# A decoder trunk on one core: gated-branch and merge-gate chunks of the in-projection as seven block products, the recurrence on 128-channel tiles, and the second branch product first

## The chip, the cores and the metric

The kernel runs on one core of a Trainium2 chip. The metric is the device time of one execution in microseconds, as the median of several runs. A profile of one further execution, taken by the hardware, gives the time of every instruction on every engine: TensorE (PE, and PEld for its weight loads), VectorE (DVE), ScalarE (ACT), GpSimd (POOL) and the queues of the DMA engines, of which SP's and POOL's are used here.

## The reference

One layer, 1024 positions, width 1024, everything in float32. Three branches come out of one wide in-projection; the rest is an output projection and a squared-ReLU MLP.

```python
h = rms_norm(x, g_mix)
z = einsum("bsd,de->bse", h, w_in) + b_in                # 1024 -> 7168
va, ga, xb, gb, sa, sb = split(z)                        # 1024,1024,1536,1536,1024,1024
u = causal_depthwise_conv(va * sigmoid(ga), conv_a_w, conv_a_b)      # width 31
u = silu(layer_norm(u, ln_g, ln_b))
y_a = u @ w_a_out
v = causal_depthwise_conv(xb, conv_b_w, conv_b_b)                    # width 4
r, i = sigmoid(blockdiag(v, w_rg_a) + b_a), sigmoid(blockdiag(v, w_rg_x) + b_x)   # 16 heads of 96
a = exp(-8 * r * softplus(-lam))
bterm = sqrt(1 - a**2) * i * v                           # the root is 1 at position 0
hs[t] = a[t] * hs[t-1] + bterm[t]
y_b = (hs * gelu(gb)) @ w_b_out
x = x + (sigmoid(sa) * y_a + sigmoid(sb) * y_b) @ w_o
x = x + square(relu(rms_norm(x, g_mlp) @ w_1)) @ w_2
return rms_norm(x, g_final)
```

## The kernel before

Activations lie transposed: channels on the 128 partitions, positions along the row, so a tile is 128 channels by 1024 positions (4 KB per partition), and a PSUM bank takes 512 positions. Precision is kept by splitting each operand into a high part in a rounded format (float32r) and a low part, the rest; a product is then three products: high by high, high by low, low by high. `split` makes the parts with a ScalarE copy and a VectorE subtraction; `split_dma` with two ScalarE copies and an accumulating transfer on POOL's queue.

**In-projection.** The 7168 output channels are 56 chunks of 128. `zchunk` loads the chunk's weights (`get_w`, two buffers each of raw, high and low), and `mm3` runs 8 blocks x 3 parts x 2 halves = 48 products of 128x128 by 128x512 into one of three PSUM tiles of two banks. The first three chunks are made beside the first normalization (`first_z`). The order of the others is the order of the program: for j from 0 to 7, three `xb` chunks (while j is below 4), one `va` and one `ga` chunk (`va_pair`), and some merge-gate chunks (`GATES`); then the 12 gated-branch chunks `GB`. `step()` after a chunk advances the recurrence by one unit.

**Recurrence.** A unit is one head (96 channels) and one half of the positions (32 units): `rnn_load` gathers its 96 rows out of the 128-channel tiles by SP's queue, `rnn_split` makes the parts, `rnn_gates` runs 6 products into one PSUM tile (both gates, one half each) and two sigmoids, and `rnn_scan`, per head, does Exp, Tanh and Sqrt on ScalarE and multiplications and the scan on VectorE, and sends the rows back to the 128-channel tile by SP's queue.

**Long convolution.** In `va_pair`, 30 taps of one VectorE instruction each per chunk (L508, with 1024 positions), at a priority lowered by 1500 so that they fill VectorE's gaps.

**After the in-projection.** The layer norm over the eight convolution tiles is spread over the `GB` loop (`layer_norm_steps`, at `LNS`); a `GB` chunk's Gelu is multiplied straight into the recurrence's tile. Then come the first branch product, `ya` (8 chunks of 48), and the second, `yb` (8 chunks of 72), each multiplied by merge gates that lay in DRAM (`spill`); the output projection; the MLP. The MLP's up-projection (`up_mm`, `up_step`) already takes its 2x2 block products by a scheme of seven instead of eight (Strassen's, in Winograd's form), 12 products a step, on a pool of eight single PSUM banks; so does the down-projection.

**Order.** Except where `tc.manual_schedule` fixes the order of PE, ACT and DVE (start, head of the MLP, down-projection), a scheduler lays down each engine's order before the run, by priority (earlier in the program first, `tc.high_priority` ahead), and each engine then runs its queue strictly in that order. Tiles come from pools with a fixed number of slots; `acts`, the largest, has 35 tiles of 4 KB per partition. An instruction that writes a tile waits until the last reader of the slot's former tile is done.

Of the kernel before, what the change touches and what calls it, by code (L numbers as in the profile page):

```python
# [9 lines left out]
F32 = mybir.dt.float32  # L10
F32R = mybir.dt.float32r
# [14 lines left out]
QB = 11  # L26
GATES = (0, 1, 1, 2, 3, 3, 3, 3)
LNS = (3, 4, 6, 8, 9)
# [4 lines left out]
def trunk_kernel(ctx: ExitStack, tc: tile.TileContext, x, xt_in, vecs, w_in, w_a_out, w_b_out,  # L33
# [8 lines left out]
    wp = early.enter_context(tc.tile_pool(name="weights", bufs=2))  # L42
# [27 lines left out]
    def split_w(raw, shape, name, pool=wp, tag=None):  # L70
        wh = pool.tile(shape, F32R, tag=tag or "wh", name=name + "_h")
        wl = pool.tile(shape, F32R, tag=tag or "wl", name=name + "_l")
        split_dma(raw, wh, wl)
        return wh, wl
# [48 lines left out]
    rnn = ExitStack()  # L123
    qp = rnn.enter_context(tc.tile_pool(name="half", bufs=QB))
    vp = rnn.enter_context(tc.tile_pool(name="evac", bufs=2))
    up = rnn.enter_context(tc.tile_pool(name="conv_in", bufs=2))
    rp = rnn.enter_context(tc.tile_pool(name="heads", bufs=2))

    def Q(name, dt=F32, rows=HD):
        return qp.tile([rows, HS], dt, tag="q", name=name)  # L130

    def EV(name):
        return vp.tile([P, HS], F32, tag="ev", name=name)


    vec = cp.tile([P, 452], F32, name="vec")
# [10 lines left out]
    lam_c = vec[0:HD, 404:420]  # L147
    ba_c = vec[0:HD, 420:436]
    bx_c = vec[0:HD, 436:452]
# [34 lines left out]
    xh = [T(f"xh{c}", F32R) for c in range(8)]  # L184
    xl = [T(f"xl{c}", F32R) for c in range(8)]
# [36 lines left out]
    def x_scaled(hf, c):  # L222
        u = xc[4 * hf + c // 2][:, HALVES[c % 2]]
        nc.vector.scalar_tensor_tensor(u, u, gmix_c[:, c:c + 1], rb[hf], ALU.mult, ALU.mult)
        nc.scalar.activation(xh[c][:, HALVES[hf]], u, AF.Copy)

    def x_low(hf, c):
        u, h = xc[4 * hf + c // 2][:, HALVES[c % 2]], xh[c][:, HALVES[hf]]
        nc.vector.tensor_tensor(xl[c][:, HALVES[hf]], u, h.bitcast(F32), ALU.subtract)

    xw = [(wide(xh[k]), wide(xl[k])) for k in range(8)]
# [20 lines left out]
    def first_z(i, hf, k, which):  # L252
        w, a = {"hh": (0, xh), "lh": (1, xh), "hl": (0, xl)}[which]
        nc.tensor.matmul(z0[i][:, HALVES[hf]], w0[i][w][:, k, :], a[k][:, HALVES[hf]],  # L254
# [4 lines left out]
    c8 = cp.tile([HD, NH], F32, name="c8")  # L259
    sm = cp.tile([HD, 8, NH], F32, name="sm")  # L260
    c4 = sm[:, 7, :]

    def decay():
        smi = cp.tile([HD, NH], I32, name="smi")
# [32 lines left out]
    with tc.manual_schedule(engines={mybir.EngineType.Activation, mybir.EngineType.DVE,  # L297
                                     mybir.EngineType.PE}):
        warm = cp.tile([P, 2], F32, name="warm")
        nc.vector.memset(warm, 1.0)  # L300
# [63 lines left out]

    VA, GA, XB, GB, SA, SB = 0, 8, 16, 28, 40, 48
# [17 lines left out]
    hst = vt  # L383
# [17 lines left out]

    gws = {}
    parts = {}

    def rnn_load(hd, hf):
        g, hh = divmod(hd, 4)
        v = Q(f"v{hd}_{hf}")
        for (ti, p0, p1, d0) in PIECES[hh]:
            nc.sync.dma_start(v[d0:d0 + p1 - p0, :], vt[3 * g + ti][p0:p1, HALVES[hf]])
        parts[hd, hf] = [v]  # L410
        if hf == 0:
            raw = rp.tile([HD, 2, HD], F32, tag="rraw", name=f"rraw{hd}")
            if hd < 2:
                nc.gpsimd.tensor_copy(raw[0:1, 0, 0:1], vt[0][0:1, 0:1])
            nc.sync.dma_start(raw, w_rg[hd])
            gws[hd] = raw

    def rnn_split(hd, hf):
        if hf == 0:
            gh = rp.tile([HD, 2, HD], F32R, tag="rh", name=f"rgh{hd}")  # L420
            gl = rp.tile([HD, 2, HD], F32R, tag="rl", name=f"rgl{hd}")
            split(gws[hd], gh, gl)
            gws[hd] = (gh, gl)
        vh = Q(f"vh{hd}_{hf}", F32R)
        vl = Q(f"vl{hd}_{hf}", F32R)
        split_dma(parts[hd, hf][0], vh, vl)
        parts[hd, hf] += [vh, vl]

    def rnn_gates(hd, hf):
        v, vh, vl = parts.pop((hd, hf))  # L430
        gh, gl = gws[hd]
        ps = PS(f"rg{hd}_{hf}", "ps2")
        for gi in range(2):
            o = ps[:HD, HALVES[gi]]
            nc.tensor.matmul(o, gh[:, gi, :], vh, start=True, stop=False)  # L435
            nc.tensor.matmul(o, gl[:, gi, :], vh, start=False, stop=False)  # L436
            nc.tensor.matmul(o, gh[:, gi, :], vl, start=False, stop=True)  # L437
        r = Q(f"r{hd}_{hf}")
        i = Q(f"i{hd}_{hf}")
        nc.scalar.activation(r, ps[:HD, 0:HS], AF.Sigmoid, bias=ba_c[:, hd:hd + 1])  # L440
        nc.scalar.activation(i, ps[:HD, HS:S], AF.Sigmoid, bias=bx_c[:, hd:hd + 1])
        nc.vector.tensor_tensor(i, i, v, ALU.mult)
        return r, i

    def rnn_scan(hd, rs):
        g, hh = divmod(hd, 4)
        if hd < NH - 1:
            at = wide(T(f"a{hd}")[:HD, :])
        else:
            at = [Q(f"a{hd}_{hf}") for hf in range(2)]  # L450
        for hf in range(2):
            r = rs[hf][0]
            nc.scalar.activation(at[hf], r, AF.Exp, scale=c8[:, hd:hd + 1])
            nc.scalar.activation(r, r, AF.Tanh, scale=c4[:, hd:hd + 1])
# [834 lines left out]
```

## Time and profile before

| | |
|---|---|
| time, median of 3 runs (lowest, highest) | 1623.0 us (1622.24, 1624.71) |
| the profiled execution: its time, its span | 1622.71 us, 1620.7 us |
| TensorE products | 7074 |
| busy: PE, DVE, ACT, POOL | 1600.2, 1094.9, 931.0, 179.8 us |
| granted TensorE clock, mean | 0.999 |
| DMA: software queue, hardware queue | 97.24 MB, 147.22 MB |
| end of the in-projection; of `ya`; of `yb` | 678.6, 765.7, 897.2 us |

Busy time is the time in which an engine had at least one instruction running; TensorE's is modelled, since its products overlap in a pipeline, so the count of products in a stretch of time says more. In the window rows, each engine has its busy time and, in brackets, its instructions; then come the granted clock, the share of the 16 DMA engines and GB/s. In the rows of groups, the columns are line, engine, operation, output and inputs with shapes, and count; then busy time and mean ns of one; then the idle time of the engine just before them and what ended most of it.

### The profile page before, as it was taken

What the parts mean: (1) busy time and instruction counts of PE and PEld (TensorE: products, weight loads), DVE (VectorE), ACT (ScalarE), POOL (GpSimd) and SP (SyncE); (2) the same over time, 40 slices, a digit from 0 to 9 for tenths busy, and PEclk for the clock granted to TensorE, in tenths of its full rate; (3) what the DMA queues carried; (4) which work ended last, traced back from release to release, by engine and by line L of the source; (5) the groups of instructions that cost most, each with busy time, mean ns of one, the idle gap of its engine ahead of it and who ended that gap; (6) DMA issues with size and microseconds to landing.
All of it is one profiled execution on the core that took longest, in us unless ns stands there. A gap on an engine that the chain in (4) does not pass through costs nothing.

```text
span 1620.7 us, 18731 instructions
## 1 busy us (share of the span) xinstructions
PE 1600.2 (99%) x7074; PEld 1313.3 (81%) x7074; DVE 1094.9 (68%) x1319; ACT 931.0 (57%) x1185; POOL 179.8 (11%) x244
## 2 busy tenths in 40 slices
PE   8999999999999999999999999999999999999997
PEld 6888888888888887888888888788888888888886
DVE  6699999998989736612312146865555457888898
ACT  5579889999973347722422235654444466555552
POOL 0111111211211100111111100000000001111110
PEclk9999999999999999999999999999999999999999
DMA  7556666766664543464754641633322579889862
GB/s 291 113 127 143 141 153 137 163 152 161 166 143 119 131 92 90 111 189 98 184 137 115 181 156 66 198 116 116 115 104 104 184 231 234 214 215 228 214 130 104
DMA packets 81513, 245.90 MB, mean 152 GB/s; under 512 B 9568, under 2 KB 11104, under 8 KB 81424
## 3 DMA queue, kind: packets, MB, share of 16 engines
q0 software_dynamic: 29392, 97.24, 29.7%
q1 hardware_dynamic: 51888, 147.22, 27.4%
q8 instruction: 55, 0.90, 0.2%
q14 instruction: 34, 0.28, 0.1%
q10 hardware_dynamic: 144, 0.26, 0.0%
HBM read 123.05 MB, written 33.55 MB: 97 GB/s over the span
## 4 chain that ended last, share of the span: by engine, by line
PE 94%; issue 2%; DVE 2%; ACT 1%; DMA 1%; POOL 0%; SPq 0%; POOLq 0%; DVEq 0%; ACTq 0%
PE z L92 33%; PE d L1073 14%; PE yb L92 8%; PE ya L92 5%; PE o L672 3%; PE e L1188 2%; PE keep L1073 2%; PE o L92 2%; PE z L254 2%; PE rg L437 1%; PE rg L435 1%; DMA vl<-v 1%; PE rg L436 1%; PE o L696 1%; PE tr_m L744 0%
## 5 line engine op out<-in xcount | busy, mean ns | idle before, releaser
L508 DVE SCALAR_TENSOR_TENSOR y<-u,vec,y 128x1024 f32<-128x1024 f32 x240 | 307.3, 1281 | 15.8 <-ACT y L504 10.7
L92 PE MATMUL z<-xh,win_h 128*128 128x512 f32 x848 | 262.9, 391 | 0.0
L92 PE MATMUL z<-xl,win_h 128*128 128x512 f32 x848 | 261.8, 390 | 0.0
L92 PE MATMUL z<-xh,win_l 128*128 128x512 f32 x848 | 200.9, 389 | 0.0
L92 PEld LDWEIGHTS z<-xh,win_h 128*128 128x128 f32 x848 | 159.2, 188 | 35.8 <-issue 1.7
L92 PEld LDWEIGHTS z<-xl,win_h 128*128 128x128 f32 x848 | 159.2, 188 | 33.8 <-issue 0.2
L92 PEld LDWEIGHTS z<-xh,win_l 128*128 128x128 f32 x848 | 159.2, 188 | 33.0
L1085 DVE TENSOR_TENSOR acc<-acc,d 128x1024 f32<-128x1024 f32 x72 | 87.8, 1220 | 33.4 <-PE d L1073 32.7
L68 ACT ACTIVATE win_h<-win_raw 128x1024 fp32r<-128x1024 f32 x53 | 55.8, 1055 | 86.3 <-PE z L92 81.0
L67 POOL DMA_DIRECT2D win_l<-win_raw x53 | 46.6, 880 | 336.1 <-ACT win_l L66 299.9
L66 ACT ACTIVATE win_l<-win_raw 128x1024 fp32r<-128x1024 f32 x53 | 55.7, 1050 | 10.0 <-PE z L92 6.1
L635 DVE TENSOR_TENSOR sb<-yb,sb 128x1024 f32<-128x1024 f32 x8 | 9.8, 1224 | 73.8 <-PE yb L92 73.8
L806 ACT ACTIVATE o<-s 128x512 fp32r<-128x512 f32 x64 | 38.1, 621 | 32.6 <-DVE s L798 28.3
L611 DVE TENSOR_TENSOR m<-ya,sa 128x1024 f32<-128x1024 f32 x8 | 9.8, 1224 | 68.8 <-PE ya L92 68.8
L806 ACT ACTIVATE o<-w_raw 128x512 fp32r<-128x512 f32 x40 | 25.0, 624 | 51.4 <-DVE o L720 50.8
L590 DVE TENSOR_TENSOR v<-v,ge 128x512 f32<-128x512 f32 x24 | 16.4, 689 | 47.7 <-ACT ge L588 47.7
L397 DVE SCALAR_TENSOR_TENSOR v<-xb,vec,v 128x1023 f32<-128x1023 f32 (+2 forms) x36 | 45.4, 1272 | 2.2 <-ACT v L392 2.2
L720 DVE TENSOR_TENSOR o<-s,o 128x512 fp32r<-128x512 f32 x64 | 42.4, 685 | 5.9 <-ACT o L806 5.8
L704 DVE TENSOR_TENSOR x<-xr,o 128x1024 f32<-128x1024 f32 x8 | 9.6, 1218 | 51.9 <-PE o L672 37.7
L67 POOL DMA_DIRECT2D db_1l<-wr x7 | 6.1, 870 | 327.4 <-ACT db_1l L66 304.8
L118 ACT ACTIVATE xn<-x 128x1024 f32<-128x1024 f32 x8 | 8.4, 1057 | 58.4 <-DVE x L704 58.4
L92 PE MATMUL ya<-suh,wa_h 128*128 128x512 f32 x128 | 39.4, 389 | 0.0
(1104 smaller groups left out, 3859.5 us busy)
## 6 DMA issues: line engine op xcount, KB each, us to landing
win_raw<-in_w_in_dram SPq DMA_DIRECT2D x53, 512.0 KB, 4.8
win_l<-win_raw POOLq DMA_DIRECT2D x53, 512.0 KB, 4.6
fr<-fd SPq DMA_DIRECT2D x32, 512.0 KB, 5.6
wr<-in_w_dram SPq DMA_DIRECT2D x32, 512.0 KB, 5.9
w_raw<-in_w_dram SPq DMA_DIRECT2D x31, 512.0 KB, 3.4
gates<-s POOLq DMA_DIRECT2D x32, 256.0 KB, 4.3
fd<-fa SPq DMA_DIRECT2D x16, 512.0 KB, 3.1
fd<-fb SPq DMA_DIRECT2D x16, 512.0 KB, 3.2
```

Source lines behind the costliest of these rows:

```text
L66: nc.scalar.activation(l, src, AF.Copy, scale=-1.0)
L67: nc.gpsimd.dma_start(l, src, accum_op=ALU.add)
L68: nc.scalar.activation(h, src, AF.Copy)
L92: nc.tensor.matmul(ps[:, HALVES[hf]], a, b[hf], start=i == 0, stop=i == len(todo) - 1)
L254: nc.tensor.matmul(z0[i][:, HALVES[hf]], w0[i][w][:, k, :], a[k][:, HALVES[hf]], start=k == 0 and which == "hh", stop=k == 7 and which == ...
L397: nc.vector.scalar_tensor_tensor(v[:, d:S], a[:, 0:S - d], cbw_c[:, w * 12 + t:w * 12 + t + 1], v[:, d:S], ALU.mult, ALU.add)
L508: nc.vector.scalar_tensor_tensor(acc, u[:, w:w + S], caw[:, w * 8 + j:w * 8 + j + 1], acc, ALU.mult, ALU.add)
L672: nc.tensor.matmul(ps[:, HALVES[hf]], tok(a, k, t), wo[k][b][:, HALVES[hf]], start=k == 0 and b == 0 and n == 0, stop=k == 7 and b == 1)
L720: tt(l, src, h.bitcast(F32), ALU.subtract)
L806: nc.scalar.activation(o[:, 0], src, AF.Copy)
L1073: nc.tensor.matmul(o, a, b, start=n == 0 and (p != 1 or g == 0), stop=n == len(todo) - 1, skip_group_check=p == 1 and g > 0)
L1085: tt(acc[p, q2], acc[p, q2], ps, ALU.add)
```

## The change

The twelve gated-branch chunks and the sixteen merge-gate chunks leave the loop over j and follow it as a second stage. They are taken in 14 pairs (`ZPAIRS`): a pair of chunks, two halves of the inner dimension and two halves of the positions make a 2x2 block product, done in seven steps (`z_step`, `z_mm`) of 12 products each. The right operands are sums of blocks of the normalized x (`x_sums`), read back from a copy in DRAM (`xu`); the left ones are sums of blocks of the weights (`z_lhs`), five of seven split by `split_dma`. Sums of results are made by copying a PSUM bank into another (ScalarE) and accumulating further products there, and by VectorE additions on the way out. Gelu times the recurrence's output goes to DRAM (`hgd`), merge gates as before (`spill`). PSUM is eight single banks in this stage, and nine weight tiles are shared by raw weights and split operands.

The recurrence takes a whole head (1024 positions) as its unit for the gate products, with one PSUM tile per gate in the single `ps2` slot; the gates are gathered by SP's queue into 128-channel tiles, and the scan runs on three such tiles for four heads. The scanned tiles go to DRAM (`hd`). Five long convolutions are issued in the first stage (`CONVS`), three in the second. Then the second branch product `yb` comes first, with the layer norm spread over its chunks, and `ya` follows.

```diff
+CONVS = {0: 0, 1: 1, 2: 2, 3: 3, 5: 4}
+    xu = dp.tile([2, 4, P, S], F32, name="xu")
+    for n, a in enumerate(xc):
+        nc.sync.dma_start(xu[n // 4, n % 4], a)
...
+        for gi in range(2):
+            ps = PS(f"rg{n}_{gi}", "ps2")
+            for hf in range(2):
+                o, hs = ps[:HD, HALVES[hf]], HALVES[hf]
+                nc.tensor.matmul(o, gh[:, gi, :], vh[:, hs], start=True, stop=False)
+                nc.tensor.matmul(o, gl[:, gi, :], vh[:, hs], start=False, stop=False)
+                nc.tensor.matmul(o, gh[:, gi, :], vl[:, hs], start=False, stop=True)
+            a = H(f"g{n}_{gi}")
+            nc.scalar.activation(a, ps[:HD, :], AF.Sigmoid, bias=(ba_c, bx_c)[gi][:, n:n + 1])
+            for (ti, p0, p1, d0) in PIECES[hh]:
...
+                nc.sync.dma_start(gate[gi, t][p0:p1, :], a[d0:d0 + p1 - p0, :])
+    def rnn_scan(g):
+        tiles = range(3 * g, 3 * g + 3)
...
+        for t in tiles:
+            r = gate[0, t]
+            at[t] = T(f"a{t}")
+            nc.scalar.activation(at[t], r, AF.Exp, scale=c8[:, t:t + 1])
+            nc.scalar.activation(r, r, AF.Tanh, scale=c4[:, t:t + 1])
+        for t in tiles:
+            r = gate[0, t]
             nc.scalar.activation(r, r, AF.Sqrt)
+        for t in tiles:
+            a, r, i = at[t], gate.pop((0, t)), gate.pop((1, t))
             nc.vector.scalar_tensor_tensor(r, a, 1.0, r, ALU.add, ALU.mult)
...
+            nc.vector.tensor_tensor_scan(i, a, i, 0.0, ALU.mult, ALU.add)
+            nc.sync.dma_start(hd[t], i)
...
+    def x_sums(c2, last=()):
+        q = {}
+        for n, (hf, kk) in {12: (1, 0), 11: (0, 0), 22: (1, 1), 21: (0, 1)}.items():
+            q[n] = wp.tile([P, S], F32, tag="w", name=f"xs{n}_{c2}") if n in last else \
+                T(f"xs{n}_{c2}")
+            nc.sync.dma_start(q[n], xu[hf, 2 * kk + c2])
+        sub = nc.vector.tensor_tensor
+        sub(q[11], q[12], q[11], ALU.subtract)
+        sub(q[12], q[22], q[12], ALU.subtract)
+        sub(q[22], q[22], q[11], ALU.subtract)
+        sub(q[21], q[21], q[22], ALU.subtract)
+        for p, n in ((7, 12), (6, 22), (5, 11), (4, 21)):
+            xbh[p][c2] = h = T(f"xs{p}h_{c2}", F32R)
+            nc.scalar.activation(h, q[n], AF.Copy)
+            xbl[p][c2] = l = T(f"xs{p}l_{c2}", F32R)
+            sub(l, q[n], h.bitcast(F32), ALU.subtract)
     for j in range(8):
         if j < 4:
             for i in range(3):
                 xb_chunk(3 * j + i)
                 step()
         va_pair(j)
-        for _ in range(GATES[j]):
-            gate_chunk(gate)
...
+        if j in CONVS:
+            conv(CONVS[j])
+        if j == 6:
+            x_sums(0)
+    for _ in rnn_it:
+        pass
+    stage.close()
+    banks.close()
...
+    wp = stage.enter_context(tc.tile_pool(name="weights2", bufs=9, reuse_waits="tile"))
+    sp_ = stage.enter_context(tc.tile_pool(name="sums", bufs=4, reuse_waits="tile"))
+    vp = stage.enter_context(tc.tile_pool(name="evac", bufs=5, reuse_waits="tile"))
+    zp = banks.enter_context(tc.tile_pool(name="psum_z", bufs=8, space=bass.MemoryType.PSUM,
+                                          reuse_waits="tile"))
...
+    def z_bank(i, b):
+        zb[i, b] = t = zp.tile([P, HS], F32, tag="z", name=f"z{i}{b}")
+        if i < 2 and b in "be":
+
+            nc.tensor.matmul(t, xh[0][0][:, 0:P], xh[0][0][:, 0:HS], start=True, stop=True)
+        return t
...
+    def z_step(i, p):
+        z_mm(i, p)
+        with tc.high_priority():
+            if p == 1:
+                nc.scalar.activation(z_bank(i, "b"), zb[i, "a"], AF.Copy)
+            elif p == 6:
+                nc.scalar.activation(z_bank(i, "e"), zb[i, "b"], AF.Copy)
+                zb[i, "u"] = EV(f"zu{i}")
+                nc.scalar.activation(zb[i, "u"], zb[i, "b"], AF.Copy)
...
+    x_sums(1, (22, 21))
+    zseq = [(0, 1), (1, 1), (0, 2), (1, 2), (0, 7), (0, 6), (0, 5), (1, 7), (0, 3), (0, 4),
+            (1, 6), (1, 5)]
+    for i in range(2, NZ):
+        zseq += [(i, 1), (i - 1, 3), (i - 1, 4), (i, 7), (i, 6), (i, 2), (i, 5)]
+    zseq += [(NZ - 1, 3), (NZ - 1, 4)]
+    ready = 0
+    for n, (i, p) in enumerate(zseq):
+        while ready < min(len(zseq), n + 4):
+            if zseq[ready][1] == 1:
+                z_load(zseq[ready][0])
+            z_lhs(*zseq[ready])
+            ready += 1
+        z_step(i, p)
+        if p == 4 and i in (0, 2, 5):
+            conv({0: 5, 2: 6, 5: 7}[i])
...
+    with tc.high_priority():
+        wb0 = first_wb()
+        for t in range(12):
+            raw = T(f"hg{t}")
+            nc.sync.dma_start(raw, hgd[t])
...
+            split(raw, h, l)
+            hg.append((h, l))
...
     for j in range(8):
+        ws = wb0 if j == 0 else get_w(w_b_out[j, 0], f"wb{j}a") + get_w(w_b_out[j, 1], f"wb{j}b")
...
+        if j in (0, 3, 5):
+            next(ln_it)
```

More of the change, by code (lines that the diff above doesn't have):

```diff
@@ L445, in rnn_scan @@
[L445 to L454, printed above, removed]
-        init = 0.0
-        for hf in range(2):
-            r, i = rs[hf]
-            a = at[hf]
+    gate = {}
```

422 lines of the change are left out of this document (237 added, 185 removed).

## The prediction

> **What bounds the kernel now.** I read the page first, for the share of each engine and the granted clock.
>
> ```profile
> PE 1600.2 (99%) x7074; PEld 1313.3 (81%) x7074; DVE 1094.9 (68%) x1319; ACT 931.0 (57%) x1185; POOL 179.8 (11%) x244
> ...
> PEclk9999999999999999999999999999999999999999
> ```
>
> TensorE is busy nearly all of the time at the full clock. Busy time is modelled, so I checked the count of products against time, by the table of windows, one row for each stage:
>
> ```profile
> core 0: us, PE busy (x) PEld busy (x) DVE busy (x) ACT busy (x) POOL busy (x), PEclk, DMA share, GB/s
> 125.00:380.00 255.00, 255.00 (x1121) 206.91 (x1120) 244.77 (x251) 232.91 (x288) 43.37 (x59) 1.00 0.67 152
> 766.00:897.00 131.00, 131.00 (x575) 107.36 (x574) 37.34 (x38) 47.47 (x60) 20.40 (x26) 1.00 0.60 153
> 985.00:990.00 5.00, 3.60 (x17) 2.69 (x16) 1.22 (x1) 0.48 (x1) 0.22 (x1) 1.00 0.33 104
> 1012.00:1032.00 20.00, 17.62 (x75) 13.34 (x73) 15.88 (x20) 13.79 (x19) 1.77 (x2) 1.00 0.46 116
> 1073.00:1265.00 192.00, 192.00 (x848) 158.98 (x848) 105.55 (x166) 88.52 (x132) 0.00 (x0) 1.00 0.32 113
> 1265.00:1570.00 305.00, 305.00 (x1346) 251.96 (x1346) 233.03 (x207) 176.05 (x182) 42.33 (x49) 1.00 0.82 213
> ```
>
> 1121 products in 255 us are 227.5 ns each, 848 in 192 us are 226.4 ns, 1346 in 305 us are 226.6 ns: one pitch everywhere, so TensorE waits for nothing in these rows, although VectorE is 96% and ScalarE 91% busy in the first. It does wait at the change to the eight-bank PSUM pool (rows 985 and 1012): 1.4 + 2.4 = 3.8 us. The chain of waits in order of time gives the same pitch:
>
> ```profile
> 443.32 10.90 PE z L92 x48
> ...
> 678.62 87.04 PE ya L92 x384
> 765.66 131.55 PE yb L92 x576
> ...
> 1106.09 2.72 PE f5c L815 x12
> ```
>
> A chunk of 48 products takes 10.90 us; a step of the block scheme that the up-projection already uses, 12 products, takes 2.72. So time follows the number of products plus what TensorE is made to wait. For the other engines I read the groups of instructions, shapes kept apart:
>
> ```profile
> L508 DVE SCALAR_TENSOR_TENSOR y<-u,vec,y 128x1024 f32<-128x1024 f32 x240 | 307.3, 1281 | 15.8 <-ACT y L504 10.7
> ...
> L720 DVE TENSOR_TENSOR o<-s,o 128x512 fp32r<-128x512 f32 x64 | 42.4, 685 | 5.9 <-ACT o L806 5.8
> ...
> L53 DVE TENSOR_TENSOR hgl<-v,hgh 128x1024 fp32r<-128x1024 f32 x12 | 14.1, 1222 | 1.3 <-ACT hgh L52 1.0
> ...
> L806 ACT ACTIVATE o<-s 128x512 fp32r<-128x512 f32 x64 | 38.1, 621 | 32.6 <-DVE s L798 28.3 <-DVE s L795 3.0 <-issue 1.2
> ...
> L453 ACT ACT_TABLE_LOAD x28 | 35.9, 1283 | 0.6
> ```
>
> The last column shows why idle VectorE and ScalarE cost nothing now; the means are my prices.
>
> **Products removed.** 28 chunks (12 gated-branch, 16 merge-gate) of 48 products are 1344. As 14 pairs of 7 steps of 12 they are 1176: 168 fewer. Four products are added to initialize banks. Gate products (192), layer norm and all else keep their counts. 164 x 227 ns = 37.2 us. The Trainium skill ("TensorE: Matmul & The Clock Gate", on issue gaps) gives 215.7 ns for this size, by which it would be 35.4 us; the pitch of the trace, 226.4 to 227.5 ns, decides. The profiled execution took 1622.7 us (span 1620.7 and 2.0 around it), 0.3 below the median of the runs. Without any new wait: 1622.7 - 37.2 = 1585.5. The rest is what TensorE may now wait for.
>
> **First stage: VectorE.** It ends after 25 chunks and 16 heads of 12 products: 52 us (first three chunks) + 25 x 10.9 + 16 x 2.72 = 368 us. From 52 us, VectorE has the 36 taps of the short convolution (36 x 1.27 = 46), the recurrence on 12 wide tiles (1.22 + 1.28 + 1.22 and a scan of two halves, 2 x 1.28 by the row of the 512-wide scan: 75; before, 32 units cost 105), head weights 5, gating products 10, block sums of x 10, and five long convolutions of 30 x 1.281 (192): 338 in 316 us. The excess of 22 us is in long taps, which have the lowest priority and three convolutions left for later anyway. In the second stage VectorE has, for each pair, four sums, two low parts, two additions (8 x 0.69 = 5.5; 14 pairs: 77), 24 gating products (17), the second block sums (10), three convolutions (115) and the 22: 241 in 14 x 7 x 2.72 = 267 us. That fits; its cover is the layer norm's late place, after the fourth chunk of the second branch product (4 x 16.4 = 66 us on). I take 0.
>
> The eight copies of x to DRAM (0.5 MB each, at some 2 us of all sixteen engines) enter SP's queue near 50 us, ahead of weight loads; the DMA share from 30 to 50 us is 0.15, and two weight buffers cover them: 0.
>
> **First stage: ScalarE and the gate bank.** Grouping three tiles removes table loads: 85 in this stage now (28 + 28 + 11 + 11 + 7, 109 us). Four groups leave perhaps 16, some 20 us. This time was hidden, so it buys only slack. Against it: both gates of a head now use the one gate bank pair in turn, so the second waits for the first sigmoid (a 128x1024 eviction takes 1.1 us, with a table load 2.4) unless the order puts chunk products between. Bounds 0 and 16 x 2.4 = 38 us; the row at 125 us shows no wait in an order that the scheduler made, so nearer the lower end: 3 us. The gate tiles go back by SP's queue, ahead of weight loads queued behind them; the group write of the recurrence waits there for the scan. The cover is two weight buffers, one chunk of 10.9 us; in this row it holds. A gain is excluded, since TensorE waits for nothing there.
>
> **Change of stage.** The 8-bank pool and new weight tiles open where the last chunk still holds its weights. Step (0,1) can have operands in slots free earlier; (1,1) and (0,2) wait for the last chunk's slots, then two ScalarE copies (0.62 each) and an accumulating transfer of about 4 us (192 KB ones take 5.1). Two ready steps cover 5.4 us. Bounds 0 and 10; the nearest row is the 3.8 us above: 3 us.
>
> **Second stage.** Each pair needs on ScalarE 12 splits and 8 evictions (20 x 0.63 = 12.6) in 19.0 us, on VectorE 5.5 to 8.3, and on the queues 1.0 MB of weights, 1.3 MB of accumulating and 1.0 to 2.1 MB of other transfers: 170 to 230 GB/s, beside 213 at a DMA share of 0.82 in the row at 1265 us, without a wait. The row at 1073 us runs the same seven steps at full pitch. New are nine shared weight slots and a low part by transfer. The second raw tile of the next pair waits for the last split of this one: 8.2 us (three steps) + copy 0.7 + transfer 5 + load 5 = 19 us, just one pair; its first use is 8.2 us later. A tap in front of a sum adds 1.3. Bounds 0 and 14 x 1.3 = 18; near the row that shows none: 3 us.
>
> **Second product first.** The 12 gated tiles come back from DRAM and are split (12 x 1.22 = 14.7 us of VectorE) while the first pass over them lasts 48 x 0.227 = 10.9 us; the tiles of "acts" come free only as the last pair's operands retire, 13.6 us before the end. Missing lead 3.8 us, at worst 14.7: 3 us. Layer norm now ends against the first branch product: after the sixth chunk it has 2 x 16.4 = 33 us for reciprocal (6.7), root and eight scale, silu and split steps of some 2.7 us each, the last needed 7 us after the start: 35 of 39; 1 us.
>
> Sum: 1585.5 + 3 + 3 + 3 + 3 + 1 = 1598.5, and 0.3 to the median: 1599.
>
> **Rivals.** (1) Nothing waits: under 6 us of waits, 1586 to 1591. The row at 1073 us speaks for it, four new changes of order against it. (2) The second stage is bound by its nine slots or the gate bank binds the first: the upper ends, 18 or 20 more instead of 3, 1611 to 1621. For it: the 19 us loop; against: bank and slot slack. (3) A clock that falls: in the last 11 us of the span, where TensorE runs dry, its granted clock is 0.80. If waits at four places each brought such a stretch, 4 x 11 x (1/0.80 - 1) = 11 us more, 1610. Against it: the clock stays 1.00 in the rows at 985 and 1012 us, with waits in them. The Trainium skill ("TensorE: Matmul & The Clock Gate", on HAM oscillation) has a rule of this kind, for idle gaps over about 3.4 us; no gap inside this trace is shown to be that long. (4) Slower: the "acts" pool. A round of the first stage (five chunks, four heads) is 65 us of TensorE but 11.5 + 1.3 + 1.4 + 18.5 + 38.5 = 71 us of VectorE, and the first round has only 32; after four rounds 284 us of work met 228, so 56 us of taps are late. I count 33 to 35 of 35 tiles held then (14 of x, six branch tiles, nine of the recurrence, the rest waiting convolutions). If these run out, the lag becomes TensorE's wait: 1598.5 + 56 = 1655 in full, 1630 to 1645 if half or more is paid; the sign turns when about 25 of the 56 are. Against: branch tiles and recurrence tiles go before the taps in priority. That the products do not fall in number is excluded: the loops fix 1176.
>
> **How the numbers follow.** Forecast (1591 to 1611) 0.48; rival 1 0.15; rival 2 0.15; rival 3 0.05; rival 4 0.14, and 0.03 for landing within 0.2% (3.2 us, about what a measurement of this kernel can tell from no change). Faster 0.48 + 0.15 + 0.15 + 0.05 = 0.83. The range 1587 to 1622 leaves out rival 4 and the lowest edge of rival 1.
>
> **What would show it.** The page: 6910 TensorE products, fewer by 164. Windows: pitch near 227 ns in the second stage of 267 us and in the first; waits of a few us at its start, at its end, and nowhere else. Groups: table loads down by some 70. The waits of TensorE on the gate tiles, the block weights and the gated tiles would size 3, 3, 3. I am wrong if a window of the first 370 us shows a pitch above 240 ns, or VectorE's taps end later than 66 us into the second branch product.

## The result, and the profile after

The changed kernel takes 1699.0 us (median of 4 runs, 1695.45 to 1702.45) against 1623.7 us before in the same comparison: a ratio of 1.0464, 95% interval 1.0441 to 1.0488. The forecast was 1599, with 1622 as the upper end, so both the direction and the range were wrong; the time also lies above every time that the four rivals named, of which 1655 was the highest. The profiled execution took 1702.45 us, its span 1700.6.

The page first: the shares of the engines and the granted clock in 40 slices.

```profile
PE 1601.7 (94%) x6910; PEld 1298.6 (76%) x6910; DVE 1146.5 (67%) x1329; ACT 891.1 (52%) x1157; POOL 214.5 (13%) x284
...
PEclk9989999999899999989999999999999999999999
```

There are 164 products fewer, as forecast, and yet TensorE's busy time is the same, in a span 80 us longer. The second line says why busy time can't be trusted here: some slices are below 9, so products ran at a lower clock and lasted longer. The windows place it; the columns are those of before, with the rows at the first stage, the second stage, the second branch product and a part of the MLP that nothing has touched:

```profile
52.00:427.40 375.40, 335.94 (x1390) 264.63 (x1389) 302.34 (x270) 239.22 (x236) 35.22 (x43) 0.95 0.70 172
427.40:733.80 306.40, 280.93 (x1180) 224.82 (x1181) 226.78 (x253) 169.91 (x292) 91.77 (x124) 0.97 0.69 182
733.80:887.00 153.20, 140.49 (x585) 111.95 (x583) 69.19 (x55) 56.04 (x60) 21.88 (x31) 0.97 0.54 150
...
1155.00:1382.00 227.00, 227.00 (x1003) 187.94 (x1003) 118.76 (x182) 105.06 (x152) 1.72 (x2) 1.00 0.37 129
```

1390 products in 375.4 us are 270 ns each, 1180 in 306.4 are 260 ns, 585 in 153.2 are 262 ns; in the MLP it is still 226 ns. The first stage was to end at 368 us and ends at 427; the second was to take 267 us and takes 306; the second branch product took 131 us and takes 154. VectorE is busy 81% and ScalarE 64% in the first row, less than the 96% and 91% of before: no other engine has become full. The waits of TensorE, in us in total, times and longest, by the same four stretches (52 to 420, 420 to 445, 445 to 731, 731 to 890 us):

```profile
PE rg L446 <- DMA vl<-v: 31.9, 12, 5.2
...
PE z1a L632 <- ACT zo L68: 7.3, 1, 7.3
PE z0a L632 <- DVE u L501: 7.0, 1, 7.0
...
PE z1e L632 <- ACT z1e L658: 3.1, 1, 3.1
PE z6e L632 <- ACT zc L665: 3.0, 1, 3.0
PE z4e L632 <- ACT zc L665: 2.5, 1, 2.5
...
PE yb L92 <- ACT hgh L52: 4.4, 2, 3.2
PE ya L92 <- ACT suh L52: 3.4, 1, 3.4
PE yb L92 <- ACT wb1a_h L68: 2.1, 1, 2.1
```

The largest is the third product of a head's gates, which waits for the low part `vl` that `split_dma` makes by an accumulating transfer. The lists of DMA issues (queue, count, KB each, median us from issue to landing) show what became of that transfer, before and after:

```profile
vl<-v POOLq DMA_DIRECT2D x32, 192.0 KB, 5.1
```

```profile
vl<-v POOLq DMA_DIRECT2D x16, 384.0 KB, 6.7
```

It is one transfer for a head where it was two halves, and in the median it lands 1.6 us later. Its lead became shorter at the same time. I call lead the time from the issue to where TensorE would have come to the product without a wait; by the starts of the products it was 5.0 to 8.5 us before (median 7.4, without the first unit), and after it is 3.3 to 5.7 us (median 4.0) for the twelve heads of sixteen that TensorE waited for. TensorE in order of time around the longest of these waits (start, duration, line, operation, count; in brackets the idle time before it):

```profile
223.95 3.79 PE L92 MATMUL z<-xh,win_l 128*128 128x512 f32 x16
227.58 0.40 PE L444 MATMUL rg<-vh,rgh 96*96 96x512 f32 x1
227.82 0.40 PE L445 MATMUL rg<-vh,rgl 96*96 96x512 f32 x1
233.46 0.74 PE L446 MATMUL rg<-vl,rgh 96*96 96x512 f32 x1 [5.25 <-DMA vl<-v]
234.00 0.63 PE L444 MATMUL rg<-vh,rgh 96*96 96x512 f32 x1
234.43 0.63 PE L445 MATMUL rg<-vh,rgl 96*96 96x512 f32 x1
```

This transfer was issued at 224.6 us, 3 us ahead of the first of the two products that need no `vl`, and took 8.8 us. ScalarE shows why the issue was no earlier (start, duration, line, operation):

```profile
222.24 1.11 ACT L448 ACTIVATE g<-rg,vec 96x1024 f32<-96x1024 f32 x1
223.25 1.05 ACT L66 ACTIVATE vl<-v 96x1024 fp32r<-96x1024 f32 x1
```

The copy that has to precede the transfer (L66) stands in ScalarE's queue behind the second gate's sigmoid of the head before (L448). An estimate from the issues, landings and starts of all heads says that it took both, the later landing and the shorter lead: with the leads of now and the landing of 5.1 us of before, the heads would wait 10.7 us in all; with the lead of 7.4 us of before and the landings of now, 4.9 us; with both as they are, 33.4 us.

Behind the wait a product lasts 0.63 us instead of 0.40 and the next starts 0.43 us later instead of 0.23: the granted clock is 0.5 from 233.3 us for 3.4 us. The kernel before shows such a stretch only after its last product. This one has 15 of them between 100 and 892 us, 75 us in all.

I then took every start of a product from the trace. What a distance between two starts has above 227.5 ns is excess; what products have inside a half-clock stretch is put down to the clock, the rest to waits:

| us of excess | first stage | second stage | `yb` | rest | all |
|---|---|---|---|---|---|
| before | 5.4 (whole in-projection) | | 1.0 | 8.6 | 15.0 |
| after: waits | 44.8 | 31.4 | 17.9 | 8.9 | 103.0 |
| after: half clock | 15.6 | 7.4 | 4.4 | 1.5 | 28.9 |
| after: both | 60.4 | 38.8 | 22.3 | 10.4 | 131.9 |

131.9 - 15.0 = 116.9 us came in, 164 x 0.227 = 37.2 us went out: +79.7, and the spans differ by 1700.6 - 1620.7 = 79.9. So the products did give what was forecast, and everything else is waiting and the clock that follows it.

### The profile page after: what moved, and what is told of

Its sections match the earlier page's. It is cut to its first block, busy times and chain, and to the rows that moved or that the text cites. A ratio compares the mean times of both kernels' runs of the same rounds, so it can differ in the third digit from the quotient of the medians.

```text
span 1700.6 us, 18626 instructions
## 1 busy us (share of the span) xinstructions
PE 1601.7 (94%) x6910; PEld 1298.6 (76%) x6910; DVE 1146.5 (67%) x1329; ACT 891.1 (52%) x1157; POOL 214.5 (13%) x284
## 5 line engine op out<-in xcount | busy, mean ns | idle before, releaser
L516 DVE SCALAR_TENSOR_TENSOR y<-u,vec,y 128x1023 f32<-128x1023 f32 (+14 forms) x240 | 303.8, 1266 | 14.3 <-ACT y L513 10.2
L92 PE MATMUL z<-xh,win_h 128*128 128x512 f32 x400 | 131.0, 408 | 0.0
L92 PE MATMUL z<-xl,win_h 128*128 128x512 f32 x400 | 129.2, 403 | 0.0
L1244 DVE TENSOR_TENSOR acc<-acc,d 128x1024 f32<-128x1024 f32 x72 | 87.8, 1220 | 33.4 <-PE d L1232 32.8
L92 PE MATMUL z<-xh,win_l 128*128 128x512 f32 x400 | 94.8, 389 | 0.0
L92 PEld LDWEIGHTS z<-xh,win_h 128*128 128x128 f32 x400 | 79.6, 199 | 18.5 <-issue 0.2
L92 PEld LDWEIGHTS z<-xl,win_h 128*128 128x128 f32 x400 | 79.0, 197 | 18.1
L92 PEld LDWEIGHTS z<-xh,win_l 128*128 128x128 f32 x400 | 75.1, 188 | 15.6
L448 ACT ACTIVATE g<-rg,vec 96x1024 f32<-96x1024 f32 x32 | 35.6, 1112 | 65.1 <-PE rg L446 61.4
L446 PE MATMUL rg<-vl,rgh 96*96 96x512 f32 x64 | 29.2, 456 | 31.9 <-DMA vl<-v 31.9
L67 POOL DMA_DIRECT2D zo<-zw x42 | 37.1, 884 | 88.8 <-ACT zo L66 86.1
L863 DVE TENSOR_TENSOR x<-xr,o 128x1024 f32<-128x1024 f32 x8 | 9.7, 1219 | 51.4 <-PE o L831 37.2
L92 PE MATMUL ya<-suh,wa_h 128*128 128x512 f32 x128 | 40.0, 398 | 3.4 <-ACT suh L52 3.4
```

What stands on the lines that cost most here:

```text
L67: nc.gpsimd.dma_start(l, src, accum_op=ALU.add)
L92: nc.tensor.matmul(ps[:, HALVES[hf]], a, b[hf], start=i == 0, stop=i == len(todo) - 1)
L446: nc.tensor.matmul(o, gh[:, gi, :], vl[:, hs], start=False, stop=True)
L448: nc.scalar.activation(a, ps[:HD, :], AF.Sigmoid, bias=(ba_c, bx_c)[gi][:, n:n + 1])
L516: nc.vector.scalar_tensor_tensor(acc[:, d:S], u[:, 0:S - d], tap(d), acc[:, d:S], ALU.mult, ALU.add)
L1244: tt(acc[p, q2], acc[p, q2], ps, ALU.add)
```

## Experiments

The theory (A in the expectations) was that three orderings of queues cost the time, each for a part of its own: the low part of a head by transfer; two of the seven steps' operands by transfer in the second stage; the gated tiles on SP's queue. The rivals (B) put the time down to something that the edit does not touch: VectorE, the slots, DMA traffic as such. Ratios are to the kernel before, with 95% intervals.

**1. The low part of a head by VectorE.**

```diff
-        split_dma(parts[n], vh, vl)
+        split(parts[n], vh, vl)
```

> The changed kernel with one edit: the low part of a head's v is made by a VectorE subtraction instead of the accumulating transfer on POOL's queue. Theory A (the first stage waits for that transfer: 32 us of TensorE's waits and 37 us of its weight loads' waits end with it, and the clock falls behind the longer ones): the wait on the transfer is gone, the granted clock in the first stage returns from 0.95 to about 1.00, the first stage (52 to 427 us) shortens by 40 to 55 us, and the whole time falls from 1699 to 1645 to 1660 us. Rival B (VectorE bounds the first stage, 302 of 375 us busy, and TensorE's waits are its lateness passed on): the edit adds 16 x 1.2 = 19 us of VectorE work, the waits move to other releasers and the time stays within 1690 to 1715 us.

1664.9 us, 1.0257 (1.0238 to 1.0276): 34 us faster than the changed kernel. The largest waits of TensorE from 52 to 420 us, a window that now takes in the change of stage (the first two rows):

```profile
PE z0a L632 <- DVE u L501: 7.3, 1, 7.3
PE z1a L632 <- ACT zo L68: 5.9, 1, 5.9
PE rg L444 <- ACT g L448: 3.0, 2, 2.1
PE rg L446 <- DVE vl L53: 2.5, 2, 2.2
```

Of 31.9 us of waiting for `vl`, 2.5 are left, though VectorE has 16 subtractions more. The excess of the stage falls from 60.4 to 21.1, its half-clock part from 15.6 to 3.0. Making the low part without the transfer takes 39 of these 60 us away; not all of it is seen in the total, where the profiled spans differ by 38 us and the medians by 34.

**2. The gated tiles by POOL's queue.**

```diff
-            nc.sync.dma_start(raw, hgd[t])
+            nc.gpsimd.dma_start(raw, hgd[t])
```

> The changed kernel with one edit: the twelve loads of the gated tiles (hg) are issued on POOL's queue instead of SP's. Theory A (at the start of the second branch product six of the loads stand in SP's queue behind two weight loads that wait for their buffers, from 726 to 744 us): the two waits on hgh (1.4 and 3.3 us) and the half-clock stretches at 738 and 752 us go, second branch product 154 us -> 138 to 146, time 1685 to 1693. Rival B (the tiles of the large pool come free too late, or ScalarE and VectorE can't split twelve tiles fast enough): no change beyond 4 us, 1695 to 1703.

1694.2 us, 1.0431 (1.0389 to 1.0473), 4.8 us less, which is not clear of the noise: the interval of the changed kernel begins at 1.0441. The second branch product goes from 154 to 151 us: the queue is at most a small part of its 22 us.

**3. Steps 2 and 4 split by ScalarE and VectorE.**

```diff
-        if p in (7, 3):
+        if p in (7, 3, 2, 4):
             nc.scalar.activation(o[:, 0], src, AF.Copy)
             nc.vector.tensor_tensor(o[:, 1], src, o[:, 0].bitcast(F32), ALU.subtract)
```

> The changed kernel with one edit: in the second stage, steps 2 and 4, the last readers of the two raw weight tiles, make their low part by a VectorE subtraction instead of the accumulating transfer (14 x 2 more VectorE instructions, 19 us). Theory A (the raw weights of the next pair come late because SP's queue waits 120 us in all for those transfers to give the slots back, ScalarE's queue then stands with a split that waits for the raw tile, and bank evictions behind it make TensorE wait): TensorE's waits in the second stage on ScalarE evictions fall from about 17 us to under 8, the stage from 306 to 288 to 298 us, time 1680 to 1692. Rival B (VectorE is short in the second stage, 227 of 306 us busy with taps in front of the additions): the waits stay or grow, time 1696 to 1712.

1683.3 us, 1.0383 (1.0357 to 1.0408). The second stage falls from 306 to 286 us, its excess from 38.8 to 18.1. What TensorE waited for there was ScalarE, but ScalarE was 55% busy; what it waited for itself, from 445 to 712 us, points to the cause. The changed kernel, and then this one:

```profile
ACT zo L66 <- DMA zw<-in_w_in_dram: 28.5, 9, 4.4
ACT zo L66 <- DMA zo<-zw: 26.3, 10, 4.8
```

```profile
ACT zo L611 <- DVE zo L612: 19.2, 11, 2.9
...
ACT zo L66 <- DVE zo L612: 10.5, 7, 2.4
...
ACT zo L66 <- DMA zw<-in_w_in_dram: 3.4, 3, 1.6
```

A copy that waits for a slot (held by an accumulating transfer `zo<-zw`) or for a raw weight that came late into its own slot stands in ScalarE's queue ahead of the bank copies (`zc`, `z1e`) that the next step needs. With fewer transfers the slots come free sooner; the wait for `zo<-zw` is no longer among the seven largest. ScalarE still waits 29.7 us, now for VectorE's subtractions, but in pieces of at most 2.9 us, and TensorE's waits for ScalarE from 445 to 712 us fall from 16.5 to 3.3 us.

**4. Work of no use in front of the wait.** Ten products with zero weights per head, before the first that needs `vl` (160 in all): 36 us more of TensorE.

```diff
+    zero = cp.tile([HD, HD], F32R, name="zero")
+    nc.scalar.activation(zero, ident[:HD, :HD], AF.Copy, scale=0.0)
...
                 nc.tensor.matmul(o, gl[:, gi, :], vh[:, hs], start=False, stop=False)
+                if gi == 0 and hf == 0:
+                    for _ in range(10):
+                        nc.tensor.matmul(o, zero, vh[:, hs], start=False, stop=False)
```

> The changed kernel with ten products with an all-zero weight tile put into each head's first gate, between its second product and the first one that needs the low part of v: 160 products of 227 ns, 36 us more work, which adds zero to the result. Theory A (waits near and over 3 us lower the granted clock for stretches of 3.4 us and multiples, 29 us lost in all, 16 of them in the first stage): the fill takes the place of most of the waits, so that the half-clock stretches of the first stage mostly go; 36 of work, less about 27 of wait that it covers, less 10 to 16 of clock: time 1688 to 1702, granted clock in the first stage 0.99 to 1.00. Rival B (the clock is not lowered by waiting but by something else, load or time): granted clock stays near 0.95 and the time is 1704 to 1716. Rival C (zero products do not count as activity): as B, with the clock falling at the same places.

1696.9 us, 1.0459 (1.0444 to 1.0475), level with the changed kernel in spite of 36.4 us more work. The wait for `vl` falls from 31.9 to 5.2 us, the half-clock part of the stage from 15.6 to 1.5. The transfer takes no less time (8.2 us in the median); TensorE only has something to do. So what matters is whether the lead covers the landing, and part of the price of a wait is the clock behind it.

**5. The three edits together, and without two thirds of the taps.** In the second run the long convolution has 10 instead of 30 taps on VectorE; the rest of its sum is left out.

```diff
-            for d in range(1, WA):
+            for d in range(1, 11):
```

> The changed kernel with the three edits of the first runs together (v's low part by VectorE, low parts of steps 2 and 4 by VectorE, gated tiles loaded by POOL's queue). Theory A (three separate losses that add): 1699 - 34 - 16 - 5 = 1644, 1638 to 1650. Rival B (VectorE, which takes on 38 us of work for them, has become the bound of both stages): 1655 to 1670, with the second stage back over 300 us.

> The three edits, and the long convolution with 10 instead of 30 taps on VectorE (20 x 8 instructions, 203 us of VectorE work, and with them that part of the convolution, are left out). Theory A (what still waits in the first stage and where the stages meet, about 18 + 18 us with its share of the clock, is VectorE behind time, with taps in front of the operations that TensorE needs): first stage 336 to 318 to 324 us, the two waits at the start of the second stage (7.5 and 6.2 us) under 4 in sum, time 1644 to 1605 to 1620. Rival B (the order of the queues and the late slots, not VectorE's load): 1636 to 1646, waits at the same places.

The three together: 1642.8 us, 1.0118 (1.0103 to 1.0133). Alone they gave 34.1, 4.8 and 15.7, in sum 54.6; together 56.2, so the three losses add up, as separate causes would. With 203 us of VectorE left out it is 1627.7, 1.0031 (1.0021 to 1.0041): 15 us. The excess of the first stage is 16.5 instead of 21.6, of the second 14.3 instead of 20.5, of `yb` 17.7 instead of 19.6. VectorE's load has a share then, but it is no bound: 48.5 of the 61.7 us of excess in these stages stay without it.

**6. Three convolutions in the first stage, five in the second** (on the three edits).

```diff
-CONVS = {0: 0, 1: 1, 2: 2, 3: 3, 5: 4}
+CONVS = {0: 0, 1: 1, 2: 2}
...
-        if p == 4 and i in (0, 2, 5):
-            conv({0: 5, 2: 6, 5: 7}[i])
+        if p == 4 and i in (0, 1, 3, 5, 7):
+            conv({0: 3, 1: 4, 3: 5, 5: 6, 7: 7}[i])
```

> The three edits, and two of the five long convolutions of the first stage issued in the second stage (three in the first, five in the second), nothing left out. Theory A (VectorE short in the first stage, with room in the second): the first stage and the stage boundary lose 10 to 20 us of their waits, the layer norm comes late by less, time 1625 to 1640. Rival B (taps fill only gaps, so that where they are issued does not matter, and the load is the same in sum): 1640 to 1650, or slower when the layer norm is late at the first branch product.

1644.2 us, 1.0127 (1.0112 to 1.0142), no gain. The excess of the second stage falls from 20.5 to 10.8 and that of `yb` rises from 19.6 to 30.2: the VectorE work that was put off meets the splits of the gated tiles (TensorE now waits 3.8 us for `hgl` on VectorE, and 5.4 us for `wb1a_h` where it was 3.1).

**7. Half of the gated tiles** (on the changed kernel). The last six are neither loaded nor split; the first six are used twice.

```diff
+            if t > 5:
+                hg.append(hg[t - 6])
+                continue
```

> The changed kernel with one edit: at the second branch product the last six gated tiles are not loaded and split, and the first six stand in for them (six loads of 512 KB, six copies, six subtractions and the use of their data are left out); TensorE has the same products. Theory A (the tiles that come free late, and the loads and splits that wait for them, cost this stage its 15 us of waits at its head and the clock behind them): second branch product 154 us -> 138 to 143, time 1683 to 1690. Rival B (the weights of the branch product, one buffer behind, are what is late): 150 to 154, time 1693 to 1702.

1691.5 us, `yb` 147 us instead of 154. Late tiles are one third of its excess of 22.3 (7.1 us); weights that are late too (`wb1a_h` 2.1 us, `wb7a_l` 2.9 us) stay.

**8. Three orders at the two changes of stage** (each on the three edits, 1642.8): the block sums of x loaded by POOL's queue; the raw weights of the first two pairs loaded ahead of the second block sums; and three orders in the second branch product: its first chunk taken tile by tile, its last chunk no longer so, and the second and third part of the layer norm one chunk earlier.

```diff
-            nc.sync.dma_start(q[n], xu[hf, 2 * kk + c2])
+            nc.gpsimd.dma_start(q[n], xu[hf, 2 * kk + c2])
...
+    z_load(0)
+    z_load(1)
     x_sums(1, (22, 21))
...
-        if j < 7:
+        if j > 0:
             mm3(ps, ops)
-        if j in (0, 3, 5):
+        if j in (0, 2, 4):
```

> The three edits, and the eight loads of x blocks (xs) are issued on POOL's queue instead of SP's. Theory A (at the stage boundary SP's queue stands for 16 us with xs loads that wait for their slots, and the first raw weights behind them come late): the wait before the first product of the second stage (7.4 us) and the next (6.1 us) fall to under 5 in sum, and the clock does not fall there: time 1643 to 1625 to 1634. Rival B (VectorE, whose last u product and block sums stand behind taps, holds the boundary): 1638 to 1646, waits at the same two places.

> The three edits, and the raw weights of the first two pairs are loaded ahead of the second set of x blocks in the program (order alone). Theory A (as for the run before: the weights' place in SP's queue): time 1625 to 1634. Rival B (VectorE holds the boundary): 1638 to 1646. Rival C (the weights take slots that the x blocks need, and the block sums become late instead): waits move to the steps that need them, 1640 to 1655.

> The three edits, and in the second branch product the first chunk takes its three products tile by tile (six products a tile instead of four in the first pass, so a tile is needed every 1.36 us instead of 0.91), the last chunk takes the ordinary order, and the layer norm's three parts come after chunks 0, 2 and 4 instead of 0, 3 and 5. Theory A (the head of this stage waits for gated tiles, its end for low parts of the last weights and for the layer norm): stage 152 us -> 140 to 146, time 1631 to 1638. Rival B (the first weights wb1a and the tiles arrive too late for any order): 148 to 154, time 1640 to 1646.

The first two: 1639.2 (1.0097; 1.0082 to 1.0112) and 1642.3 (1.0121; 1.0104 to 1.0138). Neither takes the wait of about 7 us at the change of stage away. It is not a transfer: the first product of a pair needs a bank whose last reader is the product `u` on VectorE (L501), and in VectorE's fixed queue that stands behind taps. VectorE in the changed kernel, in order of time:

```profile
419.75 1.22 DVE L548 TENSOR_TENSOR xs4l<-xs,xs4h 128x1024 fp32r<-128x1024 f32 x1
420.88 5.18 DVE L516 SCALAR_TENSOR_TENSOR y<-u,vec,y 128x1013 f32<-128x1013 f32 x4
425.98 1.28 DVE L501 SCALAR_TENSOR_TENSOR u<-z,vec,u 128x1024 f32<-128x1024 f32 x1
```

TensorE stood from 420.1 to 427.4; ScalarE's part of `u` was done at 421.6, so some 4.4 us of this are the four taps. `u` is not the only holder: without two thirds of the taps (experiment 5) its wait is gone, and one of 8.0 us for `zo` on ScalarE stands in its place. The third, 1635.5 (1.0079; 1.0062 to 1.0097), gives 7 us: `yb` goes from 152 to 145 us, its excess from 19.6 to 12.7.

**9. Five edits together** (1, 2, 3, the weights first, the order of `yb`), with four or three convolutions in the first stage, and the four with the second gate's PSUM tile taken from the chunks' banks.

```diff
-CONVS = {0: 0, 1: 1, 2: 2, 3: 3, 5: 4}
+CONVS = {0: 0, 1: 1, 2: 2, 4: 3}
...
-            ps = PS(f"rg{n}_{gi}", "ps2")
+            ps = PS(f"rg{n}_{gi}", ("ps2", "ps")[gi])
```

> The three edits, the raw weights ahead of the second x blocks, the orders in the second branch product, and four long convolutions issued in the first stage instead of five. Theory A (the boundary is held twice, by VectorE's last u product behind taps and by the raw weights in SP's queue, so either edit alone leaves the other): the boundary's waits fall from 13 us to under 4, stage one loses 3 us, and with the 8 of the order edits the time is 1612 to 1624. Rival B (one holder alone, which neither edit reached, such as the PSUM bank of the last chunk): waits of 10 to 14 us remain there, time 1626 to 1636.

> As the run before with three long convolutions in the first stage and five in the second. Theory A: the boundary's waits under 4 us as there, but VectorE's taps run into the second branch product and the gated tiles' low parts come behind them, 5 to 12 us there: time 1618 to 1632, slower than with four. Rival B: the boundary keeps 10 us or more, 1630 to 1640.

> As the run with four convolutions, and the second gate of a head takes a PSUM tile from the chunks' three instead of the single gate slot. Theory A (the forecast's rival 2: the one gate slot costs 4 to 6 us of TensorE's waits on the first sigmoid in the first stage): those waits go, 3 to 6 us faster than the run with four convolutions. Rival B (three tiles for chunks and gates are too few): new waits of chunk products on evictions, 0 to 15 us slower.

Four convolutions: 1625.5 us, 1.0017 (1.0008 to 1.0027). Three: 1627.3, 1.0026 (1.0017 to 1.0035). With the gate banks: 1636.5, 1.0086 (1.0071 to 1.0101); the chunks then wait for the sigmoids (`PE z L92 <- ACT g L448`, 14.1 us in 4 waits), so the single pair of gate banks was the better choice. The windows of the first of them:

```profile
52.00:386.00 334.00, 320.03 (x1395) 255.88 (x1394) 302.35 (x278) 225.32 (x223) 22.89 (x28) 0.99 0.68 176
386.00:669.00 283.00, 273.24 (x1181) 221.08 (x1180) 258.41 (x294) 155.31 (x261) 68.37 (x100) 0.99 0.59 166
669.00:812.00 143.00, 136.31 (x585) 110.14 (x583) 69.76 (x56) 58.20 (x62) 25.68 (x38) 0.99 0.58 165
```

239, 240 and 244 ns for a product: 73 us are won back from the changed kernel, and some 45 us of excess are left in these three stages.

**10. The two largest waits that were left.** The weights of the second chunk of `yb` ahead of the gated tiles; and that with the fourth convolution issued between the stages.

```diff
         wb0 = first_wb()
+        wb1 = get_w(w_b_out[1, 0], "wb1a") + get_w(w_b_out[1, 1], "wb1b")
...
+    conv(3)
     x_sums(1, (22, 21))
```

> The kernel with five edits and four long convolutions in the first stage (1625.6 us), plus one: the second chunk's weights of the second branch product are loaded and split ahead of the gated tiles instead of behind them. There TensorE waits 4.7 us for wb1a_h, whose ScalarE copies stand behind a copy of a gated tile that waits for its transfer. Theory A (order of ScalarE's queue): the wait goes, 1619 to 1622, level with the kernel before or just below. Rival B (the gated tiles are then late by the same): 1624 to 1628.

> As the kernel with the weights ahead, and the fourth convolution issued at the start of the second stage instead of inside the first. At the change of stage TensorE waits 7.8 us for a product u on VectorE that stands behind four taps of that convolution (379.1 to 384.2 us); with three convolutions in the first stage this wait was 2.6 us, but the second branch product then paid 7.4 us more. Theory A (both are queue order): the wait falls to under 3 us and the second branch product keeps its 11 us, 1614 to 1619, faster than before. Rival B (VectorE's work of the second stage ends too late): 1622 to 1628.

The first: 1624.3 us, 1.0010 (1.0000 to 1.0019). Its wait did not move, though:

```profile
PE z0a L632 <- DVE u L501: 7.4, 1, 7.4
...
PE yb L92 <- ACT wb1a_h L68: 4.6, 1, 4.6
```

The edit missed its aim; the 1 us between the two runs is within the noise. The second: 1634.9, 1.0074 (1.0057 to 1.0090). The wait for `u` is gone, but others of 5.9 us (for the bank copy `z0b` on ScalarE) and 3.4 us (for `zo`) came in its place, and the convolution that starts later again costs the second stage and `yb` (excess 24.4 and 19.7). No version beat the kernel before; the best is 0.1% above it, which can't be told from level.

## Why the prediction was wrong

**Products: right.** 6910 of them, 37.2 us less, at an unchanged pitch where nothing waits. The table loads fell by 61, from 99 to 38, where some 70 were forecast, and as forecast this bought only slack.

**"First stage: ScalarE and the gate bank ... 3 us": the step that failed most.** It asked whether the second gate waits for the first sigmoid. It hardly does (0.2 us in the profile after, 3.0 where experiment 1 has taken the longer wait away). What it left out is in the prediction's own list of changes: a unit is a whole head now, so the transfer for `vl` is twice as large, and the order gives it less lead than before. The row of 5.1 us for 192 KB was used only for the change of stage. The term was 60.4 - 7.0 = 53.4 us: 31.9 of direct wait, 15.6 of half clock, the rest small. Experiment 1 gives 34 us for this one line. "TensorE waits for nothing there" was true of an order whose lead was 7.4 us in the median against a landing of 5.1, and even there three of the 32 transfers made TensorE 0.1 to 0.3 us late; a row without a wait says nothing of how thin its cover is. Which weighs more, the later landing or the shorter lead, no run separates; the estimate above needs both.

**"First stage: VectorE ... 0": wrong, but small.** Without two thirds of the taps the first stage still had 16.5 of 21.6 us.

**"Change of stage ... 3 us", bounds 0 and 10: mis-sized.** It measured 7.0 + 7.3 = 14.3 us of waiting, and the clock was halved for 17 of the 21 us from 424 to 445, which cost 4.4 us more. It named weights and slots, which are the second wait; the first, for a bank held until VectorE's queue reaches `u` behind taps, was not thought of.

**"Second stage ... 3 us", bounds 0 and 18: mis-sized.** 38.8 - 7.3 - 4.4 = 27.1 us, of which 3.0 are half clock. The loop through the slots, which the step itself worked out, was real: experiment 3 takes 20.7 us of the stage's excess away. I chose the end near the MLP's row, in which the same seven steps run at pitch; that row has neither shared slots nor five operands of seven made by transfer, so it was the wrong neighbour.

**"Second product first ... 3 + 1 us": mis-sized.** 22.3 us instead of 1.0 before; 7.1 us go with half of the gated tiles (experiment 7), and 7 us with three edits of the order (experiment 8), in part perhaps the same 7; late weights are among the rest. How the whole divides was not shown.

**Rivals.** Rival 3, the clock, had a chance of 0.05 and a price of 11 us; it came in addition to every other term and cost 28.9. It rested on four waits; there were fifteen stretches. Rival 4 had the right sign for another reason. It put the loss down to taps that run out of tiles, but the transfer `vl` makes 31.9 of the 32.6 us that TensorE waits in the first stage up to 420 us, and leaving two thirds of the taps out gave 15 us. Rival 2 was right on the slots and wrong on the gate bank. Of the two signs of being wrong, the first came (272 ns a product from 52 to 370 us) and the second did not: the last tap ended at 665.5 us, 68 us before the second branch product began. The common fault is that the covers were weighed by the load of an engine, and were lost to single transfers and to the position of single instructions in a fixed queue.

**What stays open.** About 45 us of excess are left in the three stages of the best version (1624.3 us): 25 in nine waits of 1 to 7.5 us, the rest in distances that are less than 1 us too long. For the longest wait the position of `u` behind taps was seen, but every order that moved it paid elsewhere; whether an order exists that pays none was not shown.

## What to carry to other kernels

When a change doubles the unit of some work, list each transfer that grows with it and compare its landing time with its lead in the queue, transfer by transfer: here a landing 1.6 us later and a lead of 4.0 us instead of 7.4 (medians) cost 34 us in a kernel whose engines had room. An order without waits may be one without slack, so count the lead before writing 0. Where TensorE is the bound, price a wait of 2 us or more at its own length and, by the table below, a likely stretch of lower clock behind it.

## What the runs showed of the hardware

The clock falls after much shorter waits than I had assumed. In all 18 profiles I took each distance between two starts of products that was more than 1 us above 227.5 ns, behind 52 us and not begun at half clock, and noted whether a half-clock stretch began between its start and 5 us behind its end. A short wait close to a long one is counted with the fall that followed both.

| length of the wait, us | followed by half clock |
|---|---|
| 1.0 to 1.5 | 6 of 83 |
| 1.5 to 2.0 | 9 of 70 |
| 2.0 to 2.6 | 36 of 57 |
| 2.6 to 3.2 | 23 of 27 |
| over 3.2 | 65 of 65 |

A stretch lasts 3.4 us or a multiple of it (up to 13.7 us), at 0.5; the 75 us of the changed kernel cost 28.9. In the kernel before, the longest such wait was 1.6 us, and its clock never fell before the last product. The Trainium skill ("TensorE: Matmul & The Clock Gate", on HAM oscillation) warns of idle gaps over about 3.4 us, with the same half clock; all waits over 3.2 us here agree with it, but waits of 2.0 to 2.6 us were followed by a fall in over half of the cases, so its bound is not a safe one in this kernel.

Neither size nor kind ordered the accumulating transfers. Of `vl`, 192 KB landed in 5.1 us in the median and 384 KB in 6.7 (8.9 at most). But in the profile after, the 384 KB ones of the second branch product's weights (`wb1a_l` to `wb7b_l`) took 3.8 to 8.1 us, with ten of the fourteen under 4.6, the 512 KB ones of the first stage's weights (`win_l`) 4.9 in the median, and the 256 KB ones of the second stage (`zo<-zw`) 3.6. What sets these times no run shows, so a price is best taken from the row of the same tile, with its neighbours kept as bounds.
